# A decoder layer in float32: the embedding's product moved ahead of the up projection, and sixteen tiles used twice

## The chip, the core and the metric

The kernel runs on one core of a Trainium2 chip. Its engines work side by side, each through a list of instructions of its own: TensorE (PE) multiplies matrices, with weight loads shown apart as PEld; VectorE (DVE), ScalarE (ACT) and GpSimd (POOL) work on elements; SyncE (SP) starts transfers, and ACT starts some too. An instruction waits until what it needs has been produced and until the place it writes is free. On chip the data lie in 128 partitions: SBUF for operands, PSUM in eight banks for the sums of PE. The metric is the time of one execution on the device in microseconds, the median of several; a profiled execution gives the trace.

## What is computed

One layer of a decoder trunk over 1024 positions and 1024 channels: a mixer of three head groups, a gated feed-forward part, an embedding gated into the stream, and norms:

```python
h = h + jnp.concatenate([o_a, o_b.astype(o_a.dtype), o_c.astype(o_a.dtype)], axis=-1) @ w_out[l]
h = h + conv_glu_ffn(rmsnorm(h, norm_ffn_g[l]), ffn_up[l], ffn_conv_w[l], ffn_conv_b[l], ffn_down[l])
gate = jax.nn.sigmoid(rmsnorm(h, norm_ple_g[l]) @ ple_gate[l])
h = h + gate * (p[l] @ ple_proj[l])
```

`conv_glu_ffn` projects up to 2 x 2816 columns, runs a causal convolution of width 3, multiplies the SiLU of one half with the other half, and projects down. `p[l] @ ple_proj[l]`, the embedding's product (256 channels to 1024), depends on nothing that the layer computes; the last line alone needs it.

## The kernel before

All data are float32, with channels on partitions and positions along the free axis, in two halves of 512 positions (`hf` 0 and 1). Each operand of a product is split into a rounded high part and the rest as a low part (`split2`, `split_x`, `op_split`: a cast on ACT, a subtraction on DVE or POOL), and each product is three matmuls: high by high, high by low, low by high (`mm3`, L127, L129, L131; `mul`, L1094). A matmul takes 128x128 weights and 512 moving columns.

The kernel is a sequence of stages, written with pools of tiles. A pool's tiles take addresses in SBUF from the lower side, or, with `side="right"`, from the upper side. A tile that lies over an older one waits for the last use of that one. A planner of the language puts the instructions of each engine into their final order from the order of the program, the dependencies and its own idea of their durations; on the chip each engine then keeps that order. The stages that the change touches:

- **Out projection** (`phase_out`). The mixer's output stands split in the X tiles (32 of 512 columns, both halves, one pool `x`). For each half and each of eight row blocks m, the weights are loaded through the ring `wraw` (two slots, shared), split, and multiplied (`dense`, 24 matmuls to a half). DVE adds the sum to h (L1073), ACT stores it (L1074), ACT squares it and DVE adds the squares to `acc` (`sq_acc`, L185 to L189). Row blocks 0 and 1 do both halves at once. After each half `rstd_bcast` adds up over partitions by small matmuls (L159), takes the power -1/2 on POOL (L167) and spreads the result by transposes into a PSUM tile (L169).
- **Passage** (`ffn_norm`, `ffn_operands`). The up projection works by a scheme that replaces eight block products by seven, so its moving operands are seven sets of four blocks, p1 to p7, each split in high and low: p1 and p2 are the first half of the normalised h; the others are sums and differences of all blocks. `ffn_norm` scales both halves (L1122) and splits p1 and p2 (L1112, L1113). Their tiles, pool `tx`, lie where the X tiles were. `ffn_operands` loads the weights of the first two units, loads and splits the embedding's inputs through `wraw` (L1143 to L1148), multiplies p1 for two units (bank tiles `bg`), copies the result to `e` (L1201), multiplies p2 on top, and then computes the embedding's product in eight blocks of 12 matmuls (bank tiles `bv`), each copied to SBUF (L1167) and stored to memory (`ped`, L1168). Behind these in the program stand the sums and splits of p6, p5, p7 (L1175 to L1189), and of p3 and p4, whose pool `ty` lies over the embedding's tiles.
- **Up projection** (`phase_up`). 22 units, each with the products p6, p4, p5, p2, p7, p3 and p1 in pairs; its results are convolved, gated and stored.
- **Down projection** (`phase_down`). Seven products of eleven steps by the same scheme. Each step loads a block (`xs`, six tiles), splits it into two of eight tiles `xb` (dx in the profile), and takes weights (`S`, `W1`, `W2`). They all lie in pools opened when the up projection's are closed.
- **Last stage** (`ple_norm`, `phase_ple`). The gate's product, eight row blocks by two halves, with the first half's operands in a pool on the upper side and the second half's on the lower. Each row block reads back its part of `ped`.

Of the kernel before, what the change touches and what calls it, by code (L numbers as in the profile page):

```python
# [18 lines left out]
P = 128  # L19
# [60 lines left out]
class Trunk:  # L80
# [57 lines left out]
    def xall(self):  # L138

        X = [({}, {}) for _ in range(ND)]  # L140
        for h in (1, 0):
            for k in range(ND):
                X[k][0][h] = self.xpool.tile([P, HT], F32R, tag=f"xh{k}_{h}", name=self.nm("xh"), bufs=1)
                X[k][1][h] = self.xpool.tile([P, HT], F32R, tag=f"xl{k}_{h}", name=self.nm("xl"), bufs=1)
        return X
# [54 lines left out]
    def build(self):  # L200
        tc, nc = self.tc, self.nc
        with ExitStack() as st:
# [5 lines left out]
            mix, psm = ExitStack(), ExitStack()  # L208
            self.xpool = mix.enter_context(self.pool("x"))
# [15 lines left out]
            with self.pool("fps", bufs=2, space=PSUM) as self.fps:  # L225
                self.ffn_operands(hs, up)
                self.phase_up()
                up.close()
                with ExitStack() as ple:
# [824 lines left out]
    def phase_out(self, hp, op):  # L1054
# [5 lines left out]
        pbs = []  # L1060
        for hf in (0, 1):
            sl = slice(hf * HT, (hf + 1) * HT)
            acc = op.tile([P, HT], F32, tag="acc", name=self.nm("acc"))
            for m in range(ND):
                t = self.h[m][:, sl]
                if m > 1 or hf == 0:
                    w = self.load_w(self.a["w_out"][m])
                    ps = self.dps.tile([P, T], F32, tag="dp", name=self.nm("dp"))
                    halves = (0, 1) if m < 2 else (hf,)
                    self.dense([ps[:, :HT], ps[:, HT:]], w, self.O, (6, 7, 0, 1, 4, 2, 3, 5), halves)  # L1070
                    for g in halves:
                        u = self.h[m][:, g * HT:(g + 1) * HT]
                        nc.vector.tensor_tensor(u, u, ps[:, g * HT:(g + 1) * HT], ALU.add)  # L1073
                        nc.scalar.dma_start(self.hd[m][g], u)  # L1074
                self.sq_acc(acc, t, m == 0)
            pbs.append(self.rstd_bcast(acc, 1.0 / 1024, EPS, self.mxp))
        return pbs
# [37 lines left out]
    def ffn_norm(self, pbs):  # L1115

        self.TX = {}
        self.op_tiles(self.tpool, "p7", "p6", "p1", "p2", "p5")
        for hf in (0, 1):
            for k in (0, 1, 2, 3, 4, 5, 6, 7) if hf == 0 else (0, 4, 1, 5, 2, 6, 3, 7):  # L1120
                t = self.h[k][:, hf * HT:(hf + 1) * HT]
                self.nc.vector.scalar_tensor_tensor(t, t, self.par[:, PC_FFN + k:PC_FFN + k + 1], pbs[hf],  # L1122
                                                    ALU.mult, ALU.mult)
                if hf == 0:
                    self.op_split("p2" if k >= 4 else "p1", k % 4, t)

    def ffn_operands(self, hs, up):


# [3 lines left out]
        self.units = [{"f": f} for f in range(NFF)]  # L1133
        first = self.units[:2]
        for d in first:
            d["raw"], d["rav"] = self.load_up(d["f"]), self.load_up(NFF + d["f"])
            d["w1"] = self.split2(d["raw"][:, :HT], V)
        with self.pool("pe") as pp:
            pX, pw = [], []
            for k in (0, 1):  # L1140
# [416 lines left out]
```

## Time and profile before

| | us |
|---|---|
| three executions | 1567.61, 1567.92, 1576.19 |
| their median | 1567.92 |
| the profiled execution | 1568.74 |
| its span, first to last instruction | 1567.0 |

The profile shows one execution. Its page has the busy time of each engine and its share of the span. The timeline has a line for each run of like instructions: start, duration, engine (a q behind it marks the queue that issues transfers), the line in the source, output and inputs by the program's names, size and count, and in brackets how long the engine had stood idle and what ended that. PE's matmuls overlap: each is shown with 0.39 us, and at full pace one starts every 0.2267 us, so pace is read from starts. In the view by stretches each line has the stretch, its length, the busy time of PE, PEld, DVE, ACT and POOL with the number of instructions, the TensorE clock that was granted (1.00 is full), the share of time that DMA was busy, and GB/s.

### The profile page before, as it was taken

What the parts mean: (1) busy time and instruction counts of PE and PEld (TensorE: products, weight loads), DVE (VectorE), ACT (ScalarE), POOL (GpSimd) and SP (SyncE); (2) the same over time, 40 slices, a digit from 0 to 9 for tenths busy, and PEclk for the clock granted to TensorE, in tenths of its full rate; (3) what the DMA queues carried; (4) which work ended last, traced back from release to release, by engine and by line L of the source; (5) the groups of instructions that cost most, each with busy time, mean ns of one, the idle gap of its engine ahead of it and who ended that gap; (6) DMA issues with size and microseconds to landing.
All of it is one profiled execution on the core that took longest, in us unless ns stands there. A gap on an engine that the chain in (4) does not pass through costs nothing.

```text
span 1567.0 us, 20112 instructions
## 1 busy us (share of the span) xinstructions
PE 1488.1 (95%) x7480; PEld 1225.3 (78%) x7480; DVE 1098.7 (70%) x1578; ACT 631.1 (40%) x1079; POOL 430.5 (27%) x353
## 2 busy tenths in 40 slices
PE   7999999999999988999889999999999999999995
PEld 5778988788877777777768888888888778888774
DVE  6567542756556568844758888888888789867584
ACT  6522421312324455523445444444444444455541
POOL 2233220313211123213124455444454000002230
PEclk9999999989999999999989999999999999999998
DMA  5124002124043032054332333333331793352352
GB/s 193 58 88 121 28 28 81 41 74 108 1 147 103 28 108 75 28 202 148 121 120 95 101 104 111 103 103 108 107 111 70 251 329 106 112 156 61 101 175 81
DMA packets 78707, 167.84 MB, mean 107 GB/s; under 512 B 19920, under 2 KB 20048, under 8 KB 78608
## 3 DMA queue, kind: packets, MB, share of 16 engines
q1 hardware_dynamic: 65120, 145.97, 28.7%
q10 hardware_dynamic: 12400, 16.52, 3.1%
q0 software_dynamic: 1088, 4.06, 0.8%
q8 instruction: 59, 0.97, 0.3%
q14 instruction: 40, 0.33, 0.1%
HBM read 120.12 MB, written 46.40 MB: 106 GB/s over the span
## 4 chain that ended last, share of the span: by engine, by line
PE 67%; issue 18%; DVE 8%; ACT 3%; DMA 2%; POOL 1%; POOLq 0%; SPq 0%; ACTq 0%; DVEq 0%
PE bg L1094 15%; PE bv L1094 11%; PE dp L131 6%; PE dp L129 6%; PE dp L127 6%; PE hsc L849 1%; PE swq L993 1%; PE pgm L743 1%; PE bv L131 1%; PE bv L129 1%; PE bv L127 1%; PE sc L560 1%; PE swt L1016 1%; PE swo L1029 1%; PE px L736 1%
## 5 line engine op out<-in xcount | busy, mean ns | idle before, releaser
L127 PE MATMUL dp<-xh,whi 128*128 128x512 f32 x544 | 185.3, 399 | 12.7 <-ACT xh L344 8.6
L129 PE MATMUL dp<-xl,whi 128*128 128x512 f32 x544 | 186.0, 399 | 0.4 <-DVE xl L345 0.3
L131 PE MATMUL dp<-xh,wlo 128*128 128x512 f32 x544 | 184.2, 397 | 1.0 <-POOL wlo L106 1.0
L106 POOL TENSOR_TENSOR wlo<-raw,whi 128x512 fp32r<-128x512 f32 x84 | 134.9, 1623 | 92.8 <-ACT whi L104 92.7
L104 ACT CAST whi<-wraw 128x512 fp32r<-128x512 f32 x120 | 73.2, 619 | 210.4 <-PE dp L129 144.5
L106 POOL TENSOR_TENSOR wlo<-wraw,whi 128x512 fp32r<-128x512 f32 x60 | 82.5, 1375 | 269.7 <-ACT whi L104 253.2
L127 PEld LDWEIGHTS dp<-xh,whi 128*128 128x128 f32 x544 | 102.4, 190 | 36.0 <-ACT xh L344 8.6
L131 PEld LDWEIGHTS dp<-xh,wlo 128*128 128x128 f32 x544 | 103.4, 191 | 23.4 <-POOL wlo L106 1.9
L129 PEld LDWEIGHTS dp<-xl,whi 128*128 128x128 f32 x544 | 102.7, 190 | 24.3 <-DVE xl L345 2.6
L106 POOL TENSOR_TENSOR wlo<-s,whi 128x512 fp32r<-128x512 f32 x44 | 68.3, 1552 | 163.2 <-ACT whi L104 148.9
L1403 PE MATMUL bg<-dx,whi 128*128 128x512 f32 x308 | 96.6, 394 | 1.7 <-DVE dx L1400 1.5
L1403 PE MATMUL bv<-dx,whi 128*128 128x512 f32 x308 | 95.0, 390 | 0.0
L104 ACT CAST whi<-raw 128x512 fp32r<-128x512 f32 x88 | 52.5, 619 | 100.6 <-issue 51.1
L104 ACT CAST whi<-s 128x512 fp32r<-128x512 f32 x66 | 39.0, 620 | 115.3 <-PE bg L1094 112.1
L106 DVE TENSOR_TENSOR wlo<-wraw,whi 128x512 fp32r<-128x512 f32 x60 | 46.5, 780 | 49.1 <-ACT whi L104 44.3
L167 POOL TENSOR_TENSOR rst<-rst,mhalf 128x4 f32<-128x4 f32 x8 | 9.3, 1160 | 255.6 <-DVE rst L161 255.6
L1403 PEld LDWEIGHTS bg<-dx,whi 128*128 128x128 f32 x308 | 56.8, 188 | 17.5 <-ACT whi L104 4.1
L1403 PEld LDWEIGHTS bv<-dx,whi 128*128 128x128 f32 x308 | 57.8, 188 | 12.2
L1399 ACT CAST dx<-xraw 128x512 fp32r<-128x512 f32 x77 | 47.9, 622 | 46.1 <-PE bv L1403 24.8
L1400 DVE TENSOR_TENSOR dx<-xraw,dx 128x512 fp32r<-128x512 f32 x77 | 54.8, 712 | 3.0 <-ACT dx L1399 2.7
L1403 PE MATMUL bg<-dx,wlo 128*128 128x512 f32 x154 | 47.5, 390 | 1.1 <-DVE wlo L106 1.1
L286 DVE TENSOR_TENSOR dp<-dp,rstd 128x512 f32<-128x512 f32 (+1 forms) x26 | 23.3, 898 | 35.5 <-PE dp L131 25.5
(404 smaller groups left out, 3874.6 us busy)
## 6 DMA issues: line engine op xcount, KB each, us to landing
raw<-in_ffn_up_dram SPq DMA_DIRECT2D x44, 512.0 KB, 3.7
wraw<-in_w_in_dram SPq DMA_DIRECT2D x30, 512.0 KB, 3.7
z<-zst SPq DMA_DIRECT2D x18, 512.0 KB, 3.1
gb<-ct SPq DMA_DIRECT2D x33, 256.0 KB, 2.0
xraw<-gb SPq DMA_DIRECT2D x33, 256.0 KB, 2.9
xraw<-gt SPq DMA_DIRECT2D x33, 256.0 KB, 2.7
zl<-z SPq DMA_DIRECT2D x16, 512.0 KB, 3.9
wraw<-in_ple_gate_dram SPq DMA_DIRECT2D x16, 512.0 KB, 3.6
```

Of the source, the lines that this page charges most:

```text
L104: nc.scalar.copy(hi, src)
L106: eng.tensor_tensor(lo, src, hi.bitcast(F32), ALU.subtract)
L127: nc.tensor.matmul(ps[hf], wh, xh[hf], start=first, stop=False)
L129: nc.tensor.matmul(ps[hf], wh, xl[hf], start=False, stop=False)
L131: nc.tensor.matmul(ps[hf], wl, xh[hf], start=False, stop=last)
L286: self.nc.vector.tensor_tensor(ps, ps, r, ALU.mult)
L560: nc.tensor.matmul(ps[:, u, :], bb[:, u, :, :].rearrange("p a b -> p (a b)"), d["ar"][:, 4 * g + u, 0, :], start=True, stop=True)
L736: nc.tensor.matmul(px[:, u, :], U[:, 2 * hh + u, :], Xr[:, 2 * hh + u, :], start=True, stop=True)
L1094: nc.tensor.matmul(ps, w[part == 2][:, s], X[k][part == 1], start=start and k == part == 0, stop=k == 3 and part == 2, skip_group_check=no ...
L1399: nc.scalar.copy(xh, x)
L1400: V.tensor_tensor(xl, x, xh.bitcast(F32), ALU.subtract)
L1403: nc.tensor.matmul(ps[m], wt[part == 2][:, m * P:(m + 1) * P], (xh, xl)[part == 1], start=k == part == 0, stop=k == NK - 1 and part == 2)
```

## The change

**Pools.** The X tiles get one pool for each half, `x1` below `x0`. On the upper side a tile of 24 floats, `edge`, comes first, and a pool `t16` of sixteen tiles of 512 columns next; all other pools of the upper side follow behind them, lower than before.

```diff
-            self.xpool = mix.enter_context(self.pool("x"))
+            psm = ExitStack()
+            mix = [ExitStack(), ExitStack()]
+            self.xpool = [None, mix[1].enter_context(self.pool("x1"))]
+            self.xpool[0] = mix[0].enter_context(self.pool("x0"))
...
+            e(self.pool("edge", side="right")).tile([P, 24], F32, name="edge")
+            self.t16 = e(self.pool("t16", side="right"))
             up, hs = ExitStack(), ExitStack()
...
-            pbs = self.phase_out(hp, mix.enter_context(self.pool("acc")))
-            mix.close()
-            self.tpool = up.enter_context(self.pool("tx"))
-            self.ffn_norm(pbs)
+            emb = ExitStack()
+            self.pxp = emb.enter_context(self.pool("px", side="right"))
+            pb = self.phase_out(hp, mix[0], emb)
+            self.ffn_norm(1, pb)
             psm.close()
+            for n, ks in (("p6", range(4)), ("p5", range(4, ND))):
+                self.TX[n] = [[self.xpool[1].tile([P, HT], F32R, tag=f"x{c}{k}", name=f"t{n}{c}{k}", bufs=1) for c in "hl"]
+                              for k in ks]
```

**Tiles by generations.** p1 and p2 lie in `t16`, p6 and p5 in the second half's X tiles. In the down projection the sixteen tiles are used again: p1's for the six `xs` and for `S[0]`, `S[1]`, p2's for the eight `xb`.

```diff
+        xs = [self.tile16(i, F32) for i in range(6)]
+        S = {k: self.tile16(6 + k, F32) for k in (0, 1)}
+        xb = [self.tile16(8 + i, F32R) for i in range(8)]
         wa = aa.enter_context(self.pool("wa", side="right"))
-        xr = ple.enter_context(self.pool("xr"))
...
+        xl = ple.enter_context(self.pool("xl"))
+        for k in range(2, NK):
+            S[k] = xl.tile([P, HT], F32, name=f"sr{k}")
```

**Out projection.** The first half's rows come first, then one row block of the second half, then the first half's rstd. The other five row blocks of the second half have the first half's normalisation and its splits into p1 and p2 between them, two steps to a row block, and the four loads and splits of the embedding's inputs (`pe_load`), through a ring of their own with two slots. The second half's squares follow behind all rows, then its rstd, the loads of the first up weights, and five of the eight blocks of the embedding's product in the out projection's banks.

```diff
+        for m in range(ND):
+            rows(m, (0, 1) if m < 2 else (0,))
+            self.sq_acc(acc, self.h[m][:, :HT], m == 0)
+        rows(2, (1,))
+        pb = self.rstd_bcast(acc, 1.0 / 1024, EPS, self.mxp)
+        x0.close()
+        self.TX = {}
+        for i, n in enumerate(("p1", "p2")):
+            self.TX[n] = [[self.tile16(8 * i + 2 * k + c, F32R) for c in (0, 1)] for k in range(4)]
...
+        norm = self.ffn_norm(0, pb)
+        for m in range(3, ND):
+            rows(m, (1,))
+            for _ in range(2):
+                next(norm, None)
+            if parts:
+                self.pe_load(pwp, *parts.pop(0))
+        for m in range(ND):
+            self.sq_acc(acc, self.h[m][:, HT:], m == 0)
+        pb = self.rstd_bcast(acc, 1.0 / 1024, EPS, self.mxp)
+        self.ffn_first()
+        for m in range(5):
+            self.embed(m, pw, px, self.dps.tile([P, T], F32, tag="dp", name=self.nm("dp")))
+        self.pe_in = (pw, px)
+        return pb
+
+    def embed(self, m, pw, px, ps):
...
+        t = self.wpool.tile([P, T], F32, tag="wraw", name=self.nm("pst"), bufs=2)
+        self.nc.scalar.copy(t, ps)
+        self.nc.scalar.dma_start(self.ped[m], t)
...
+    def pe_load(self, raws, dst, pool, src, k):
+        raw = raws.tile([P, T], F32, tag="praw", name=self.nm("praw"), bufs=2)
+        self.nc.sync.dma_start(raw, self.a[src][k])
```

**Passage.** The sums and splits of p6 and p5 stand first, then the last three embedding blocks, then the products with p1 and p2 of the first two units; p7, p3 and p4 follow, with all three in the pool `ty`.

```diff
         for k in range(4):
             split("p5", k, B11[k])
+        for d in first:
+            d["G"] = self.banks("g")
+        for m in range(5, ND):
+            self.embed(m, *self.pe_in, self.banks("v"))
+        self.mul(*[(d["G"][:, :HT], d["w1"], self.TX["p1"], True) for d in first])
+        for d in first:
+            self.keep_first(d)
+        for d in first:
+            d["w2"] = self.split2(d["raw"][:, HT:], V)
+        self.mul(*[(d["G"][:, :HT], d["w2"], self.TX["p2"], False) for d in first])
         for k in range(4):
             V.tensor_tensor(B12[k], B22[k], B12[k], ALU.subtract)
-            split("p7", k, B12[k])
-        self.op_tiles(up.enter_context(self.pool("ty")), "p4", "p3")
...
+        emb.close()
+        pool = up.enter_context(self.pool("ty"))
+        self.op_tiles(pool, "p3", "p7", "p4")
```

The arithmetic is the same: no product, sum or transfer is added or dropped.

More of the change, by code (lines that the diff above doesn't have):

```diff
@@ L1077, in phase_out, with rows @@
-        return pbs
+        acc = hp.tile([P, HT], F32, name="acc")
+        def rows(m, halves):
+            w = self.load_w(self.a["w_out"][m])
+            ps = self.dps.tile([P, T], F32, tag="dp", name=self.nm("dp"))
+            self.dense([ps[:, :HT], ps[:, HT:]], w, self.O, (6, 7, 0, 1, 4, 2, 3, 5), halves)
+            for g in halves:
+                u = self.h[m][:, g * HT:(g + 1) * HT]
+                nc.vector.tensor_tensor(u, u, ps[:, g * HT:(g + 1) * HT], ALU.add)
+                nc.scalar.dma_start(self.hd[m][g], u)
@@ L1258, in unit @@
                 conv(prev, 0)
-            d["V"] = self.banks("v")
+            if "V" not in d:
+                d["V"] = self.banks("v")
             jobs = [(d["V"][:, :HT], ws["6"], TX["p6"], True)]
```

117 lines of the change are left out of this document (40 added, 77 removed).

## The prediction

> **What bounds the kernel now.** I read the page's shares first, then the chain of waits, then busy time by stretches, then the timeline of the stretch that stands out.
>
> ```profile
> PE 1488.1 (95%) x7480; PEld 1225.3 (78%) x7480; DVE 1098.7 (70%) x1578; ACT 631.1 (40%) x1079; POOL 430.5 (27%) x353
> ```
>
> TensorE (PE) bounds the program: a change pays only where PE stands still or runs slow. The stretches around the passage from the out projection to the up projection:
>
> ```profile
> core 0: us, PE busy (x) PEld busy (x) DVE busy (x) ACT busy (x) POOL busy (x), PEclk, DMA share, GB/s
> 742.64:769.86 27.22, 27.22 (x121) 22.34 (x119) 20.43 (x31) 13.43 (x23) 3.91 (x4) 1.00 0.45 145
> 769.86:801.25 31.39, 18.57 (x66) 14.54 (x65) 27.72 (x44) 13.19 (x24) 9.58 (x4) 0.73 0.08 25
> 801.25:822.26 21.01, 21.01 (x94) 17.43 (x93) 6.37 (x9) 9.59 (x12) 2.60 (x2) 1.00 0.57 216
> 822.26:1230.13 407.87, 407.87 (x1801) 337.46 (x1800) 355.01 (x366) 172.76 (x241) 191.50 (x123) 1.00 0.31 102
> ```
>
> The last five output rows (first line) and the whole up projection (last line: 1801 matmuls in 407.87 us, 0.2265 us each) leave PE no hole. The second line is the hole: PE busy 18.57 of 31.39 us at a granted clock of 0.73, while VectorE (DVE) works 27.72. Its timeline on PE:
>
> ```profile
> 769.63 0.39 PE L131 MATMUL dp<-xh,wlo 128*128 128x512 f32 x1
> 773.64 1.25 PE L159 MATMUL ps_ss<-few,acc 128*128 128x1 f32 x8 [3.62 <-DVE acc L189]
> 776.61 1.11 PE L169 MATMUL ps_ss<-cst,rst 128*128 128x128 f32 x4 [1.72 <-POOL rst L167]
> 777.38 1.20 PE L1094 MATMUL bg<-tp1h,whi 128*128 128x512 f32 x2
> ...
> 785.32 0.70 PE L127 MATMUL bv<-pxh,pwh 128*128 128x512 f32 x2 [0.47 <-DVE h L1122]
> ...
> 793.50 0.79 PE L1094 MATMUL bg<-tp2h,whi 128*128 128x512 f32 x1 [7.01 <-ACT e L1201]
> ...
> 801.25 0.61 PE L131 MATMUL bv<-pxh,pwl 128*128 128x512 f32 x2
> ...
> 822.10 0.39 PE L1094 MATMUL bv<-tp6h,whi 128*128 128x512 f32 x1
> ```
>
> From the last matmul of the rows (769.63) to the first with p6 (822.10) are 52.47 us. They hold that matmul, 24 with p1, 24 with p2 and 96 of the embedding: 145 x 0.2267 = 32.87. So 19.6 us are lost: the wait for the sum of squares, for the spread of rstd, for the copy of e, and matmuls at a low clock after each (p2: 24 in 7.75 us, 5.44 at full pace). Call 769.86, where the rows' last slot ends, E.
>
> **The change part by part.**
>
> *The embedding's product moves ahead, p1 and p2 behind it.* Before, p1 and p2 lie over the rows' operands, so they are split only when the rows have ended, and DVE does that ahead of the second half's normalisation:
>
> ```profile
> 775.01 2.49 DVE L1113 TENSOR_TENSOR tp1l<-h,tp1h 128x512 fp32r<-128x512 f32 x4
> 777.41 2.49 DVE L1113 TENSOR_TENSOR tp2l<-h,tp2h 128x512 fp32r<-128x512 f32 x4
> 779.82 5.34 DVE L1122 SCALAR_TENSOR_TENSOR h<-h,par,ps_ss 128x512 f32<-128x512 f32 x8
> 785.09 1.28 DVE L1179 TENSOR_TENSOR h<-h 128x512 f32<-128x512 f32 x2
> ...
> 794.72 0.68 DVE L1113 TENSOR_TENSOR tp6l<-nu,tp6h 128x512 fp32r<-128x512 f32 x1
> ```
>
> After, they have tiles of their own, and the splits run within the rows. DVE there is busy 20.43 of 27.22 us; 4.98 come in: 25.4, it still fits. Behind E: the spread arrives at 776.61 + 1.11 = E+7.9 as now, the normalisation begins at once instead of at 779.82 and ends at E+13.2, and the 10.3 us of sums and splits from 785.09 to 795.40 give p6 at E+23.5. PE has at E, ready, the five embedding blocks (60 matmuls, 13.6 us), then three more (8.2) and p1 and p2 (10.9): 32.6 us. p6 is wanted at E+32.6 at the earliest and is there 9 us before. So the filler covers the whole chain, and the 3.62 us wait goes; what is late next is not p6 but small things in PE's order, each of which I price:
>
> - *Spread of rstd.* It stays, within running matmuls. The first half's shows the cost:
>
> ```profile
> 737.81 0.39 PE L129 MATMUL dp<-xl,whi 128*128 128x512 f32 x1
> 738.04 0.94 PE L159 MATMUL ps_ss<-few,acc 128*128 128x1 f32 x8
> ...
> 740.33 0.65 PE L169 MATMUL ps_ss<-cst,rst 128*128 128x128 f32 x4 [0.76 <-POOL rst L167]
> 740.74 0.48 PE L129 MATMUL dp<-xl,whi 128*128 128x512 f32 x1
> ```
>
> Three slots after 737.81 would be 738.49; it is 740.74: 2.3 us. Without its wait of 0.76 it would be 1.5, with today's wait of 1.72 at this place 3.2. I take 2.3, the same kind of place.
>
> - *Copy of e.* It stands between p1 and p2, as before, and ACT takes its work in the order in which it was laid out:
>
> ```profile
> 785.86 1.17 ACT L1112 CAST tp5h<-h 128x512 fp32r<-128x512 f32 x2 [9.93 <-DVE h L1179]
> 792.87 1.06 ACT L1201 COPY e<-bg 128x512 f32<-128x512 f32 x2
> ```
>
> Today PE waits 7.0 us for it, because ACT stands behind casts that wait for DVE, which is late. After, p1 starts when the eight blocks are through (E + 13.6 + 8.2 + 2.3 = E+24.1) and ends at E+29.5; DVE is through p6 and p5 (E+23.5 and four more splits, 2.5) by then, so ACT should be free. The two copies alone are 1.06. From 0 (other matmuls lie between) to 7.0; I take 1.5.
>
> - *Bank of embedding block 5.* It takes a bank that the spread's result used until E+13.2; PE comes there at E+13.6+2.3. Today's wait for the same thing is 0.47 (785.32). From 0 to 3; I take 0.5.
>
> - *DVE in the rows.* The last sums of squares now stand behind all rows in the program, and 25.4 of 27.2 us is nearly full:
>
> ```profile
> L1148 DVE TENSOR_TENSOR pxl<-wraw,pxh 128x512 fp32r<-128x512 f32 x4 | 3.3, 855 | 0.0
> L1148 DVE TENSOR_TENSOR pwl<-wraw,pwh 128x512 fp32r<-128x512 f32 x4 | 2.7, 688 | 3.3 <-ACT pwh L1147 3.3
> ```
>
> The same subtraction takes 0.688 us and, where POOL is at work too, 0.855. If POOL's 3.91 us in the window came on top, DVE would be 2.1 us late at E. Up to 9 us late is covered; a matmul placed too early waits for it. From 0 to 3; I take 1.0.
>
> Sum: 2.3 + 1.5 + 0.5 + 1.0 = 5.3 us stay of 19.6. Gain 14.3.
>
> *Own loads.* The embedding's inputs leave the weights' ring for a ring of their own on the same queue (SP): the same four loads. No price; PE has no wait in those rows today. The four loads of the first up weights move too: their tiles now lie where the mix phase still works, so they leave SP after 671.47, and have some 100 us until p1 wants them. The embedding's eight copies (1.02 each) and stores sit on ACT from E on instead of from 803; ACT is busy 13.19 of the 31.39 us there, so they fit. The output tiles h lie lower in memory and may come later; today they are issued last in the mix phase:
>
> ```profile
> 671.47 1.76 SPq L1103 DMA_DIRECT2D raw<-in_ffn_up_dram  x4
> ...
> 685.70 3.94 ACTq L1059 DMA_DIRECT2D h<-in_xT_dram  x8
> 690.24 1.28 DVE L1073 TENSOR_TENSOR h<-h,dp 128x512 f32<-128x512 f32 x2 [2.67 <-PE dp L131]
> 706.58 0.50 PE L127 MATMUL dp<-xh,whi 128*128 128x512 f32 x1 [2.32 <-ACT whi L104]
> ...
> 803.26 1.02 ACT L1167 COPY pst<-bv 128x1024 f32<-128x1024 f32 x1 [0.78 <-PE bv L131]
> ```
>
> The first sum waits for PE, not for h; a delay of 2 us is hidden by the second row's matmuls, as the two rows' banks take turns. The wait at 706.58 comes from ACT's order; from 3 us less to 3 more, I take 0.
>
> *Tiles aligned.* The timeline shows a reason in the last stage, where the first half's operands lie on the upper side and the second half's on the lower:
>
> ```profile
> 1447.98:1459.22 11.24, 11.24 (x49) 9.04 (x48) 4.30 (x7) 4.38 (x6) 4.24 (x3) 1.00 0.45 148
> 1497.84:1508.49 10.65, 10.65 (x48) 8.82 (x47) 9.41 (x12) 5.02 (x9) 3.53 (x3) 1.00 0.62 210
> ```
>
> Both stretches run from one matmul's start to another's: 48 steps of 0.2342 us in the first, 47 of 0.2266 in the second, at the same clock. If the upper side's offset is the cause, 8 x 24 = 192 matmuls gain 0.0076: 1.4 us. From 0 to that; I take 1.4, since at the same clock nothing but the side differs to the first one's harm: DVE and the DMA are busier in the second.
>
> *Sixteen shared tiles.* p1 and p2 give their places to the down projection's inputs:
>
> ```profile
> 1221.75 0.39 PE L1094 MATMUL bg<-tp2h,wlo 128*128 128x512 f32 x1
> 1224.58 0.38 SPq L1397 DMA_DIRECT2D xraw<-gb  x1
> 1227.45 0.62 ACT L1399 CAST dx<-xraw 128x512 fp32r<-128x512 f32 x1 [8.40 <-DMA xraw<-gb]
> ```
>
> p2 is read last at 1221.75; the first load is issued at 1224.58 and the first cast into a shared tile stands at 1227.45, held by the load. No new wait: 0, from 1 less to 2 more.
>
> All: 14.3 + 1.4 = 15.7. The profiled execution took 1568.74 (span 1567.0), 0.8 above the median: 1553.0 by it, 1552.2 by the median, and I give that.
>
> **The rivals.**
>
> *Nothing but the spread stays.* The three small waits fall under other matmuls, and the row's wait of 2.32 goes too: 19.6 - 1.5 + 1.4 + 2.3 = 21.8, 1546.1; without the row 1548.4. For: p6 is 9 us early. Against: every in-order wait above has a precedent.
>
> *The alignment does nothing.* If the pace in the last stage has another cause than the offset, such as POOL, a little busier there (4.24 of 11.24 against 3.53 of 10.65), 14.3 remain: 1553.6. Against: in the up projection POOL is busy 191.50 of 407.87 and the pace is 0.2265. [...]
>
> *The order turns against it.* ACT again stands behind casts, e is waited for 7.0 us, and p2 runs cold (7.75 for 5.44): 2.3 + 7.0 + 2.3 + 1.0 = 12.6 stay; gain 7.0 + 1.4 = 8.4, 1559.5. For: the present order, laid out ahead by a planner, puts four embedding matmuls before p2 (785.32 to 786.5) where the wait had room for 31 more. Against: DVE is now done with those splits before p1 ends.
>
> *The alignment goes the wrong way.* If the 96 bytes put the upper side off instead of on, p1 and p2 (22 x 24 = 528), the embedding (96) and the down projection's inputs (7 x 11 x 12 = 924) run at 0.2342: 1548 x 0.0076 = 11.8 lost, nothing gained in the last stage: 1567.92 - 14.3 + 11.8 = 1565.4. The change would then not do what it says.
>
> *Slower: weights starve.* The embedding's loads have two slots; the third waits on SP until DVE has split the first, with output weights queued behind it. If each of four loads costs PE a row of 24 matmuls, 21.8 us are lost: 1567.92 - 15.7 + 21.8 = 1574.0. It decides from 3.9 us per load on. Against: the same loads pass today without a wait.
>
> **How the numbers follow.** Forecast 0.44 (own range 1549 to 1556), only the spread 0.15, alignment for nothing 0.06, the order 0.25, alignment the wrong way 0.05, starving 0.05. The range 1547.5 to 1562 leaves out half of the second case and the last two: 0.18. One per cent, about what a measurement tells from no change, is 15.7 us: 1552.2. Faster: the second case and just over half of the first (0.25), 0.40. Slower by over 1%, above 1583.6: starving half as bad again, 0.02. The rest, 0.58.
>
> **What would show it.** Embedding matmuls straight behind the last row at clock 1.0; p1 and p2 split among the rows; the normalisation right behind the spread; 0.2266 in the last stage's first half; no new wait at 1230. A wait of several us before p2 or at the sum of squares speaks for the order; any wait among the rows for starving; a pace of 0.234 in the up projection against the alignment.

## The result, and the profile after

| | before | after |
|---|---|---|
| executions | 1567.61, 1567.92, 1568.28, 1576.19 | 1551.12, 1550.87, 1548.9, 1550.8 |
| median | 1568.1 | 1550.84 |
| the profiled execution's span | 1567.0 | 1549.3 |

The ratio of the means is 0.9875 (95% interval 0.9842 to 0.9908): 1.25% less. The median is 1.4 us under the forecast of 1552.2. Where the time went is another matter. The view by stretches, cut at the same events in both kernels: the end of the mix phase, the end of the rows, the first matmul with p5, the first of the down projection, the first of the last stage, the end. Columns as in the prediction. The kernel before:

```profile
core 0: us, PE busy (x) PEld busy (x) DVE busy (x) ACT busy (x) POOL busy (x), PEclk, DMA share, GB/s
0.00:684.38 684.38, 645.56 (x3807) 536.54 (x3808) 414.18 (x716) 254.92 (x501) 170.53 (x183) 0.97 0.24 79
684.38:769.86 85.48, 81.68 (x363) 66.15 (x361) 43.15 (x63) 30.64 (x52) 16.99 (x14) 1.00 0.52 176
769.86:824.82 54.96, 42.13 (x169) 34.07 (x169) 35.04 (x55) 25.30 (x40) 12.19 (x6) 0.84 0.29 102
824.82:1230.13 405.31, 405.31 (x1789) 335.36 (x1788) 354.06 (x365) 170.24 (x238) 191.50 (x123) 1.00 0.31 102
1230.13:1447.98 217.85, 214.61 (x937) 173.75 (x937) 178.69 (x282) 106.61 (x177) 10.45 (x7) 1.00 0.53 172
1447.98:1566.97 118.99, 98.77 (x421) 79.39 (x419) 73.61 (x101) 43.42 (x74) 28.85 (x21) 0.90 0.37 121
```

The changed kernel:

```profile
0.00:679.45 679.45, 642.63 (x3807) 533.63 (x3807) 408.20 (x713) 254.82 (x501) 169.03 (x183) 0.98 0.24 78
679.45:763.04 83.59, 81.59 (x365) 66.59 (x364) 49.74 (x74) 34.97 (x60) 17.00 (x14) 1.00 0.55 193
763.04:802.84 39.80, 37.87 (x170) 30.34 (x168) 31.60 (x50) 22.39 (x35) 5.01 (x4) 1.00 0.43 152
802.84:1218.06 415.22, 413.31 (x1790) 336.71 (x1789) 362.30 (x369) 172.06 (x239) 196.79 (x126) 1.00 0.32 105
1218.06:1431.62 213.56, 213.11 (x938) 174.74 (x936) 174.83 (x275) 102.54 (x170) 10.51 (x7) 1.00 0.51 163
1431.62:1549.35 117.73, 96.70 (x421) 77.98 (x419) 73.68 (x101) 43.22 (x74) 28.90 (x21) 0.91 0.37 122
```

Line by line: mix phase -4.93, rows -1.89, passage -15.16, up projection **+9.91**, down projection -4.29, last stage -1.26; together -17.62. Behind the mix phase it is 882.59 to 869.90: -12.69, where 15.7 were forecast. The mix phase holds no edit. In the up projection PE is as full as before and has the same matmuls (1789, 1790), and still needs 413.31 us for 405.31: its matmuls are slower, and there is a hole of 1.9.

The passage on PE, in the timeline of the changed kernel:

```profile
762.81 0.39 PE L131 MATMUL dp<-xh,wlo 128*128 128x512 f32 x1
763.04 0.63 PE L127 MATMUL dp<-peh,peh 128*128 128x512 f32 x2
...
766.90 1.02 PE L159 MATMUL ps_ss<-few,acc 128*128 128x1 f32 x8 [0.48 <-DVE acc L189]
...
769.26 0.65 PE L169 MATMUL ps_ss<-cst,rst 128*128 128x128 f32 x4 [0.77 <-POOL rst L167]
...
786.42 0.74 PE L127 MATMUL bv<-peh,peh 128*128 128x512 f32 x2 [0.69 <-ACT pst L1118]
...
794.56 0.40 PE L1148 MATMUL bv<-tp6h,whi 128*128 128x512 f32 x1
...
808.06 0.39 PE L1148 MATMUL bv<-tp7h,wlo 128*128 128x512 f32 x1
810.36 0.47 PE L1148 MATMUL bg<-tp3h,whi 128*128 128x512 f32 x1 [1.91 <-ACT whi L104]
```

The embedding stands straight behind the last row; the waits of 3.62 and 7.01 are gone. New is the wait of 1.91 ahead of the first p3; behind it seven steps from start to start take 0.43 instead of 0.2267, and the granted clock from 811.90 to 815.10 is 0.50 (called half clock below). On DVE:

```profile
739.34 1.89 DVE L1167 TENSOR_TENSOR t<-h,t 128x512 fp32r<-128x512 f32 x3
...
769.95 5.36 DVE L1174 SCALAR_TENSOR_TENSOR h<-h,par,ps_ss 128x512 f32<-128x512 f32 x8 [1.83 <-PE ps_ss L169]
...
785.49 0.68 DVE L1167 TENSOR_TENSOR tp6l<-nu,tp6h 128x512 fp32r<-128x512 f32 x1
...
807.84 1.77 DVE L1262 TENSOR_TENSOR s<-s,raw 128x512 f32<-128x512 f32 x1 [1.54 <-POOL wlo L106]
809.53 0.67 DVE L1311 TENSOR_TENSOR x<-e,bg 128x512 f32<-128x512 f32 x1
```

And on ACT, the copies of the blocks 5 and 6 and the cast of p3's weights:

```profile
785.36 1.92 ACT L1118 COPY pst<-bv 128x1024 f32<-128x1024 f32 x2
...
809.70 0.62 ACT L104 CAST whi<-s 128x512 fp32r<-128x512 f32 x1 [2.14 <-DVE s L1262]
```

p1's splits run among the rows (739), the normalisation starts right behind the spread, and p6 is ready at 786.17, 23.1 us behind the rows' end (forecast 23.5); PE takes it at 794.56 (31.5, forecast 32.6).

### The profile page after: what moved, and what is told of

Its sections match the earlier page's. It is cut to its first block, busy times and chain, and to the rows that moved or that the text cites. A ratio compares the mean times of both kernels' runs of the same rounds, so it can differ in the third digit from the quotient of the medians.

```text
span 1549.3 us, 20120 instructions
## 1 busy us (share of the span) xinstructions
PE 1485.2 (96%) x7480; PEld 1220.0 (79%) x7480; DVE 1100.4 (71%) x1578; ACT 630.0 (41%) x1079; POOL 427.2 (28%) x353
## 4 chain that ended last, share of the span: by engine, by line
PE 80%; DVE 7%; issue 5%; ACT 3%; POOL 2%; DMA 2%; POOLq 0%; SPq 0%; ACTq 0%; DVEq 0%
PE bg L1148 15%; PE bv L1148 11%; PE bv L1439 7%; PE bg L1439 7%; PE dp L131 7%; PE dp L129 7%; PE dp L127 7%; PE hsc L857 2%; PE swq L1001 1%; PE pgm L751 1%; PE swo L1037 1%; PE swt L1024 1%; PE zp L127 1%; PE zp L129 1%; PE zp L131 1%
## 5 line engine op out<-in xcount | busy, mean ns | idle before, releaser
L104 ACT CAST whi<-wraw 128x512 fp32r<-128x512 f32 x120 | 73.3, 619 | 203.7 <-PE dp L129 141.7
L1148 PE MATMUL bg<-t,whi 128*128 128x512 f32 x352 | 134.3, 392 | 0.0
L1439 PE MATMUL bv<-t,whi 128*128 128x512 f32 x308 | 95.7, 392 | 0.0
L1439 PE MATMUL bg<-t,whi 128*128 128x512 f32 x308 | 95.7, 391 | 0.0
L104 ACT CAST whi<-raw 128x512 fp32r<-128x512 f32 x88 | 52.5, 618 | 98.6 <-issue 52.0
L104 ACT CAST whi<-s 128x512 fp32r<-128x512 f32 x66 | 38.8, 619 | 126.1 <-PE bg L1148 122.5
L1148 PEld LDWEIGHTS bg<-t,whi 128*128 128x128 f32 x352 | 66.2, 188 | 14.7
L1148 PE MATMUL bg<-t,wlo 128*128 128x512 f32 x176 | 67.8, 392 | 0.0
L1439 PEld LDWEIGHTS bg<-t,whi 128*128 128x128 f32 x308 | 57.8, 188 | 12.6
L1439 PEld LDWEIGHTS bv<-t,whi 128*128 128x128 f32 x308 | 57.9, 188 | 12.4
L1435 ACT CAST t<-t 128x512 fp32r<-128x512 f32 x77 | 47.7, 621 | 48.4 <-PE bv L1439 34.7
```

Of the source, the lines that this page charges most:

```text
L104: nc.scalar.copy(hi, src)
L1148: nc.tensor.matmul(ps, w[part == 2][:, s], X[k][part == 1], start=start and k == part == 0, stop=k == 3 and part == 2, skip_group_check=no ...
L1435: nc.scalar.copy(xh, x)
L1439: nc.tensor.matmul(ps[m], wt[part == 2][:, m * P:(m + 1) * P], (xh, xl)[part == 1], start=k == part == 0, stop=k == NK - 1 and part == 2)
```

## The experiments

All were timed against runs of the kernel before on the same chip. The rows come from several chips, so the ratios can be compared with each other and the medians only roughly. Since the mix phase differs from profile to profile with no edit in it, stages are compared from its end on, each from one profile. The two profiles of the changed kernel agree within 0.25 us in every stage behind it. Small differences of the last stage mean little: it takes 117.7 to 119.2 us in kernels whose first half runs at the same pace there (changed, old order).

| kernel | median, us | ratio to before (95%) | rows' end to first p5 | up | down | last | mix end to end |
|---|---|---|---|---|---|---|---|
| before | 1568.1 | 1 | 54.96 | 405.31 | 217.85 | 118.99 | 882.59 |
| changed | 1550.84 | 0.9875 (0.9842 to 0.9908) | 39.80 | 415.22 | 213.56 | 117.73 | 869.90 |
| edge of 8 floats | 1551.16 | 0.9889 (0.9855 to 0.9922) | 40.07 | 411.14 | 217.59 | 117.97 | 870.33 |
| no edge | 1557.58 | 0.9923 (0.9895 to 0.9952) | 40.18 | 415.96 | 218.47 | 117.67 | 875.89 |
| lower side 64 down | 1555.38 | 0.9897 (0.9855 to 0.9938) | 40.10 | 411.12 | 217.58 | 118.66 | 871.10 |
| before, with edge | 1567.0 | 0.9989 (0.9972 to 1.0006) | 55.83 | 405.33 | 217.82 | 118.45 | 884.51 |
| edge of 40 floats | 1542.51 | 0.9815 (0.9792 to 0.9838) | 39.57 | 409.11 | 211.49 | 117.33 | 861.17 |
| own tile for s3 | 1545.93 | 0.9829 (0.9798 to 0.9861) | 38.97 | 408.76 | 211.51 | 117.80 | 860.69 |
| old order | 1565.48 | 0.9959 (0.9942 to 0.9977) | 53.07 | 415.37 | 213.55 | 119.20 | 884.83 |
| split inputs low | 1550.44 | 0.9868 (0.9842 to 0.9894) | 39.78 | 414.24 | 211.51 | 118.87 | 867.99 |
| p6 ahead | 1546.19 | 0.9846 (0.9815 to 0.9878) | 39.55 | 407.84 | 211.51 | 118.43 | 860.98 |
| raw inputs late | 1545.54 | 0.9847 (0.9818 to 0.9876) | 39.55 | 408.11 | 212.43 | 117.50 | 861.22 |
| changed, again | 1551.26 | 0.9892 (0.9856 to 0.9927) | 39.81 | 415.20 | 213.55 | 117.98 | 870.15 |

**Where the upper side starts.** Three kernels shift one side against the other, and one gives the kernel before the edge alone.

```diff
-            e(self.pool("edge", side="right")).tile([P, 24], F32, name="edge")
+            e(self.pool("edge", side="right")).tile([P, 8], F32, name="edge")
```

> The changed kernel with the upper side pushed down by 32 bytes instead of 96: its tiles then start 64 bytes past a multiple of 128, as the lower side's tiles do, instead of on a multiple of 128. Theory A (the offset of the operands sets TensorE's pace): every step of 512 columns at 0.2267 us in the up projection (now up to 0.2314), the embedding (0.2295), the down projection (0.2287) and the last stage's first half (0.2289); about 6.6 + 0.3 + 1.9 + 0.4 = 9.2 us less, 1541.6. Theory B (operands on the upper side are slower than the old ones for another reason, such as height or the tiles' order): paces as in the changed kernel, 1550.8, within 1.

Without the edge (the line is taken out):

> The changed kernel without the 96 bytes: upper tiles start 32 bytes past a multiple of 64, as before the change. Theory A: 0.234 in the last stage's first half, as before, and now also with p1, p2 and the operands of the down projection that lie on the upper side, above 0.2314; some 6 to 9 us more, 1557 to 1560. Theory B: the last stage's first half alone goes back to 0.234 (1.0 more) and the rest stays: 1551.8.

The lower side, 64 bytes down:

```diff
-        r = self.spool.tile([P, 4], F32, tag="rst", name=self.nm("rst"), bufs=2)
+        r = self.spool.tile([P, 4], F32, tag="rst", name=self.nm("rst"), bufs=1)
...
-        r2 = self.spool.tile([P, 4], F32, tag="rst2", name=self.nm("rst2"), bufs=2)
+        r2 = self.spool.tile([P, 4], F32, tag="rst2", name=self.nm("rst2"), bufs=1)
```

> The changed kernel with one buffer instead of two for the two small tiles of rstd at the start of the lower side: everything above them on that side, the weights among it, lies 64 bytes lower and so starts on a multiple of 128, as the upper side's tiles do. Theory A1 (an operand must start 64 bytes past a multiple of 128): all streams at 0.2289 or slower, the mix phase and the rows too, 1556 or more. Theory A2 (the moving operand must have the same offset as the weights): all at 0.2267, 1541.6. Theory B: paces as in the changed kernel, 1550.8. The second rstd of a pair waits for the first; at most 0.5 us.

The kernel before, with the edge of 24 floats ahead of its upper pools:

> The kernel before with the 96 bytes alone. Both theories of the pace: the last stage's first half at 0.2289 instead of 0.2342, 1.0 us less, 1566.9; nothing else has fast operands on the upper side there. The mix phase (end of its last transposes at 684.38 before, 679.45 after the change, with no edit in it): if the 4.9 us there come from the layout of the upper side, this run shows 679.5 and some 1562; if from what is issued ahead of or behind the mix phase, or from chance in the clock, 684 and 1566.9.

None of the theories on the pace holds as it stood. The first half's 48 matmuls in the last stage of the kernel before with the edge:

```profile
1445.52:1456.50 10.98, 10.98 (x49) 9.01 (x48) 4.31 (x7) 4.38 (x6) 4.30 (x3) 1.00 0.44 146
```

0.2288 each, from 0.2342, as in the changed kernel and as both theories had it: there the edge alone sets the pace. The edge of 8 and the lowered lower side agree to 0.02 us in the up and down projections, though in one all tiles start 64 bytes past a multiple of 128 and in the other on it: the absolute start does not matter (A1 falls), nor is an equal offset modulo 128 enough (A2 falls). B falls too, as the paces change with the shift. What the two share is the distance between the sides.

**Distance 0.** The same line with 40 floats.

> The changed kernel with the upper side pushed down by 160 bytes instead of 96. The runs so far have upper tiles at these distances from the lower side's places, modulo 2048 bytes: 64 (changed kernel; up projection 0.2302 us a matmul, down 0.2288), 128 (the edge of 8 floats and the lowered lower side, alike in every stage: p1 and p2 0.234, everything else of the up projection 0.2263, down 0.2333), 160 (no edge: 0.2310, 0.2343). Here the distance is 0, as between all tiles of the lower side. Theory A, now: the distance modulo 2048 (or a divisor of it over 128) between the moving operand and the weights sets the pace, and 0 is free: 0.2267 in every stage, up projection 6 to 7 us shorter than in the changed kernel, down 1.9, last stage 0.4; 1541.5. Theory B, that operands on the upper side are slower wherever they start: p1 and p2 at 0.230 or more, 1549 to 1552.

One unit of the up projection, 84 matmuls from the first p3 to the end of p7, in the view by stretches: before, changed, and edge of 40.

```profile
920.05:939.09 19.04, 19.04 (x85) 15.77 (x84) 16.20 (x17) 7.91 (x12) 9.43 (x7) 1.00 0.26 83
```

```profile
922.42:941.76 19.34, 19.34 (x85) 15.76 (x84) 17.66 (x19) 7.90 (x12) 9.49 (x7) 1.00 0.38 123
```

```profile
921.60:940.64 19.04, 19.04 (x86) 15.77 (x84) 17.46 (x19) 7.91 (x12) 9.41 (x7) 1.00 0.37 125
```

At the same clock the changed kernel needs 0.30 us more a unit; at distance 0 that is gone, with DVE and DMA as busy as before the shift. A's forecast for distance 0 holds: 8.7 us less behind the mix phase. By its median this is the fastest kernel of the study; three kernels below that build on it lie within 0.5 us of it behind the mix phase.

**The pace by itself.** This program computes nothing of the layer: 48 matmuls for each of 17 distances, nothing beside them, then four checks of side and weights.

```diff
+        for j, (x, v, i) in enumerate(seq):
+            k = i % 4
+            nc.tensor.matmul(ps[:, j % 2 * HT:(j % 2 + 1) * HT], v[:, k * P:(k + 1) * P], x, start=j < 2,
+                             stop=j >= len(seq) - 2)
```

> A program of its own, which computes nothing of the layer: one set of 128x512 weights, and streams of 48 matmuls, each on one moving tile that starts a set distance past the weights' place modulo 2048 bytes (0 to 1984), nothing else running; at the end two tiles on the upper side (distances 0 and 64, some 210,000 bytes up), then weights 64 bytes further with the moving tiles of 64 and 0. Theory A (distance between moving tile and weights): 0.2267 at 0, about 0.229 at 64, 0.233 at 128, 0.234 at 160, slower at 64 than at 0 on the upper side too, fast again for the tile of 64 with the moved weights. Theory C (what costs is a matmul whose moving tile starts elsewhere than that of the one before it): 0.2267 in every stream but for its first step. Theory D (only with other traffic on SBUF): 0.2267 everywhere.

Its timeline: xa lies at distance 0 from wx, xb 32, xc 64, xd 96, xe 128, xf 160, xg 192, xi 256, xj 320, xk 384; xy and xz on the upper side at 0 and 64; wy 64 past wx.

```profile
62.95 11.37 PE L1614 MATMUL acc<-xb,wx 128*128 128x512 f32 x48
74.16 11.16 PE L1614 MATMUL acc<-xc,wx 128*128 128x512 f32 x48
85.15 11.37 PE L1614 MATMUL acc<-xd,wx 128*128 128x512 f32 x48
96.36 11.36 PE L1614 MATMUL acc<-xe,wx 128*128 128x512 f32 x48
107.56 11.40 PE L1614 MATMUL acc<-xf,wx 128*128 128x512 f32 x48
118.80 11.35 PE L1614 MATMUL acc<-xg,wx 128*128 128x512 f32 x48
...
141.19 11.05 PE L1614 MATMUL acc<-xi,wx 128*128 128x512 f32 x48
152.07 11.17 PE L1614 MATMUL acc<-xj,wx 128*128 128x512 f32 x48
163.07 11.32 PE L1614 MATMUL acc<-xk,wx 128*128 128x512 f32 x48
...
240.38 11.06 PE L1614 MATMUL acc<-xy,wx 128*128 128x512 f32 x48
251.28 11.17 PE L1614 MATMUL acc<-xz,wx 128*128 128x512 f32 x48
262.29 11.05 PE L1614 MATMUL acc<-xc,wy 128*128 128x512 f32 x48
273.18 11.36 PE L1614 MATMUL acc<-xa,wy 128*128 128x512 f32 x48
284.38 11.07 PE L1614 MATMUL acc<-xa,wx 128*128 128x512 f32 x48
```

From start to next start: 10.88 us at 256 (0.2267 a matmul), 11.00 at 320 and 10.99 at 64 (0.229), 11.21 at 32 (0.2335), 11.20 at 128 (0.2333), 11.24 at 160 (0.2342). The upper side is no slower than the lower (10.90 at 0, 11.01 at 64), and the tile xc, slow with wx, is fast with the moved weights (10.89). So for a stream with one moving tile it is the distance between that tile and the weights, modulo 256: A holds, D falls, and C falls as the whole cause. Stages whose moving tiles all lie at one distance show the same numbers: 160 in the last stage's first half before the change (0.2342) and in the down projection without the edge (218.47 us), 64 in the last stage's first half (0.2288) and the down projection of the changed kernel (213.56 us).

The up projection isn't given by this table. There p1 alternates with p3, and p2 with p5, and p3 to p7 stay at distance 0. A unit has 24 matmuls with p1 and p2. At the paces of the pace run they would add 0.06 us to the 19.04 of distance 0 at 64, 0.16 at 128 and 0.18 at 160. Measured are 19.34 at 64 (0.30 more), 19.21 and 19.20 at 128 (edge of 8, lowered lower side: 0.17 and 0.16) and 19.45 at 160 (no edge: 0.41). At 64, the stretches of 24 steps with p1 or p2 take 5.55 or 5.56 instead of 5.44; p6 with p4 take 5.48 instead of 5.44, and p7 2.76 instead of 2.72, though p4, p6 and p7 lie at distance 0. So the slower stream of p1 and p2 accounts for 0.06 of the 0.30 us a unit, and the edge of 8, whose distance is the slower one in the pace run, has the shorter up projection (411.14 for 415.22). Part of it may be seen in the pace run: behind a change of the moving tile a stream of 48 at distance 0 takes from 10.88 us (xi behind xh) to 10.93 (xl behind xk), up to 0.05 over 48 x 0.2267; where in the stream is not shown. So C may have a share. Why alternation costs more at 64 and 160 than at 128 stays open; that distance 0 is free (10.88 us for 48, and 19.04 a unit as before the change) is shown in both.

**The order of the filler.** All eight embedding blocks back behind p2, everything else as changed (the first five thereby move to the bank tiles of the other three).

```diff
-        for m in range(5, ND):
-            self.embed(m, *self.pe_in, self.banks("v"))
         self.mul(*[(d["G"][:, :HT], d["w1"], self.TX["p1"], True) for d in first])
...
         self.mul(*[(d["G"][:, :HT], d["w2"], self.TX["p2"], False) for d in first])
+        for m in range(ND):
+            self.embed(m, *self.pe_in, self.banks("v"))
```

> The changed kernel with its embedding blocks back behind p1 and p2, as before the change; early splits of p1 and p2, loads, tiles and alignment stay. Theory (the filler's place matters): behind the last row p1 follows, its two products end 10.9 us later, e is waited for, p6 is ready 23.5 us behind the rows at the earliest and 32.9 us of matmuls stand ahead of it, so it isn't waited for; what is lost anew is the wait for e between p1 and p2 and the clock behind it, 3 to 9 us from the rows' end to the first p5 over the 39.8 us of the changed kernel. Rival (the early splits alone did it, the place of the filler is free): 39.8 within 1.5.

53.07 us from the rows' end to the first p5 over 39.80: 13.3 lost, more than the theory asked for, and the rival falls. Its waits on PE:

```profile
766.89 1.48 PE L159 MATMUL ps_ss<-few,acc 128*128 128x1 f32 x8 [3.63 <-DVE acc L189]
769.71 1.11 PE L169 MATMUL ps_ss<-cst,rst 128*128 128x128 f32 x4 [1.34 <-POOL rst L167]
784.55 1.22 PE L1146 MATMUL bg<-t,whi 128*128 128x512 f32 x2 [5.72 <-ACT e L1234]
```

The waits of before are nearly all back. The early splits and tiles are worth 54.96 - 53.07 = 1.9 us by themselves (one profile each; the kernel before with the edge shows 55.83); the rest of the passage's gain hangs on work that is ready standing behind the rows.

**The hole ahead of p3.** The sum x reads the bank that p3 adds to, and stands on DVE behind the sum L1262 (807.84), which waits for POOL. The same sum makes p3's weights: ACT casts it from 809.70 to 810.32, x ends at 810.20, and p3 starts at 810.36. Two remedies, on the edge of 40: s3 in a tile of its own, and the second unit's p6 ahead of p3.

```diff
-                V.tensor_tensor(d["s"]["3"], d["s"]["3"], d["s"]["2"], ALU.add)
+                s3 = cv.tile([P, HT], F32, tag="s3", name=self.nm("s3"), bufs=1)
+                V.tensor_tensor(s3, d["s"]["3"], d["s"]["2"], ALU.add)
+                d["s"]["3"] = s3
```

> As the run with 160 bytes, and the third weight sum of a unit gets a tile of its own instead of being written over the sixth's. In the changed kernel the first p3 matmul stands 1.9 us behind p7 and then runs at half clock for 3 us; the sum x, which must read the bank ahead of it, stands on DVE behind that third sum, which waits for POOL to have split the sixth. Theory (order on DVE): without that wait x is done by the end of p7, the first p3 follows within 0.3 us, no half clock, 3 to 4 us less from the first p6 to the second unit's p5 than in the run with 160 bytes; some 1538. Rival (PE waits for POOL's or ACT's split of the weights themselves): the gap moves to the next product and at most 1 us goes.

```diff
+            if prev and not new:
+                d["V"] = self.banks("v")
+                self.mul((d["V"][:, :HT], ws["6"], TX["p6"], True))
```

> The run with 160 bytes, and for the second unit alone the twelve matmuls with p6 are put ahead of the first unit's p3. In the runs so far PE stands 1.7 to 1.9 us behind the first p7, because the sum x, which reads the bank that p3 adds to, comes late on DVE, behind the second unit's weight sums; a tile of its own for one of these took the wait off DVE but the sums themselves then filled the time. Theory: the second unit's p6 weights are split by the time p7 ends (POOL ends them 0.3 us before), so the twelve matmuls (2.7 us) fill the gap; x is done within them; no half clock behind. 1.9 + 1.6 = 3.5 us less than with 160 bytes alone, 1539.0. Rival: DVE is still late for what follows (p4 needs the sum behind x), and the gap moves there: 1541 to 1543.

Neither brought its 3 to 4 us (up projection 408.76 and 407.84 over 409.11). With the tile of its own DVE no longer waits, but the sums ahead of x fill the time, and PE still waits 1.72:

```profile
811.25 1.78 DVE L1257 TENSOR_TENSOR raw<-raw 128x512 f32<-128x512 f32 x1
812.95 1.77 DVE L1263 TENSOR_TENSOR s<-s,raw 128x512 f32<-128x512 f32 x1
814.64 0.67 DVE L1313 TENSOR_TENSOR x<-e,bg 128x512 f32<-128x512 f32 x1
```

With p6 ahead the hole splits in two, and the profile now names DVE:

```profile
822.21 0.50 PE L1148 MATMUL bv<-tp4h,whi 128*128 128x512 f32 x1 [1.04 <-DVE bv L1316]
...
831.57 0.47 PE L1148 MATMUL bg<-tp3h,whi 128*128 128x512 f32 x1 [0.87 <-DVE x L1314]
```

So the hole hangs on DVE's order: with p6 ahead the waits name DVE's sums, and they stand at p4 and at the next unit's p3, as the second rival had it. In the changed kernel, and with the tile of its own, two things stand between DVE's sum and p3: ACT's cast of p3's weights and x. They end within 0.12 us of each other (with the tile of its own at 815.42 and 815.31), so the runs don't tell which of them PE waits for. Of the 1.3 us that went with p6 ahead, 1.0 is the half clock's: the kernel with the raw inputs late (below) has the order of the edge of 40 in this stage and the same hole (1.94 in both), but no half clock (mean clock 1.00 over 24 us, 0.93 with the edge of 40), and takes 408.11. Against that, p6 ahead gains 0.27 and the tile of its own loses 0.65.

**The start of the down projection.** Before the change SP issued the first loads behind stores of the last units that wait for DVE:

```profile
1210.95 0.32 SPq L1312 DMA_DIRECT2D gt<-t  x1
1222.97 0.32 SPq L1298 DMA_DIRECT2D gb<-ct  x1
1224.17 0.32 SPq L1312 DMA_DIRECT2D gt<-t  x1
1224.58 0.38 SPq L1397 DMA_DIRECT2D xraw<-gb  x1
```

In the changed kernel they are issued 21 us ahead of the stage's first matmul (1218.06), not 5.6:

```profile
1197.11 0.32 SPq L1433 DMA_DIRECT2D t<-gb  x1
...
1198.97 0.86 SPq L1433 DMA_DIRECT2D t<-gb  x2
```

First, the split inputs on the lower side again:

```diff
-        xb = [self.tile16(8 + i, F32R) for i in range(8)]
+        S.update({2 + i: self.tile16(8 + i, F32) for i in range(8)})
...
+        xb = [xl.tile([P, HT], F32R, name=f"dx{i}") for i in range(8)]
```

> The changed kernel with the eight split inputs of the down projection back on the lower side, over the places of p6, and eight of its weight blocks in the sixteen shared tiles in their place. Theory A: all of the down projection at 0.2267 instead of 0.2288, 1.9 us less. Start of the stage: before the change PE waited there for the input's split 1.47 us and for the weights' 1.11, and ran cold behind; in the changed kernel it doesn't. If that came from the inputs' tiles being free early (sharing), the waits come back, 3 to 6 us, and the stage takes 214.7 to 218 us from its first matmul to the last stage's; if it came from somewhere else (loads issued earlier, DVE's order), 211.7.

211.51: the pace is back (distance 0) and no wait is. Where the split inputs lie is not the cause. Then, on the edge of 40, the raw inputs in p2's tiles:

```diff
-        xs = [self.tile16(i, F32) for i in range(6)]
+        xs = [self.tile16(8 + i, F32) for i in range(6)]
```

> The run with 160 bytes, with the sixteen shared tiles dealt out the other way: the down projection's raw inputs in p2's tiles, which the last unit reads 8.4 us before the stage, and its split inputs in p1's, which are free some 22 us before. Theory (the raw inputs' early tiles are what took the stage's first waits away): their loads are issued behind p2's last matmul, as before the change, the first splits are late again, and the down projection takes 214 to 218 us from its first matmul to the last stage's first, over 211.5 in the run with 160 bytes. Rival (the weights' early loads, or DVE's order): 211.5 within 0.7.

The loads came 12.5 us ahead of the stage (1200.43 for 1212.93), not as late as intended, and it took 212.43, 0.9 over the edge of 40. Loads 5.6 us ahead go with 6.4 lost, 12.5 with 0.9, 21 with nothing. But where the time is lost fits the raw inputs' lead only in part. Before the change the steps over 0.2267 add up to 3.5 us in the first 12 us of the stage, at two waits (1.11 for a weights' low part, 1.47 for an input's), and to 2.8 between 22 and 62 us into it, where PE waits for ACT's casts of the weights (L104). With the raw inputs late, nothing is lost in the first 22 us, and the 0.9 lies at those casts. So the weights' sums, whose loads moved too, have a share. A run with the lead of before was not made; which loads took the first two waits away stays open.

**The mix phase.**

> The changed kernel once more, unchanged. In eleven profiles of kernels with one and the same mix phase its last transposes stood between 679.45 and 688.49, with stretches of half clock of different lengths before them. If that is chance of the clock, the same kernel shows another number than its 679.45 here, anywhere up to 689, and 869.9 within 0.7 from there to the end; if it belongs to what a kernel has behind that phase, 679.45 within 0.5 again. Time 1550.8, up to 1555.

680.83 where 679.45 stood; behind it 870.15. The phase, with no edit in any of these kernels, ended between 679.45 and 688.49 (edge of 8), and at 679.46 in the kernel before with the edge alone. So its 4.93 us cannot be put down to the change. Whether the kernel before sits at 684 by chance of the clock or by something that no view shows stays open.

## Why the prediction was right, and where its sum was wrong

The time was right; the sum was right only because its errors cancel, and because the mix phase, which belongs to no step, ended 4.9 us earlier. With the mix phase of the profile before, the profiled execution would have taken 1551.12 + 4.93 = 1556.1, 3.0 over the 1553.0 that the prediction gives by the profile. That the forecast came so close is luck.

- *The filler* is the mechanism, and the runs show it (old order: 13.3 us). 19.6 us lost between the rows' end and p5 became 39.80 - 156 x 0.2267 = 4.4; 5.3 were forecast to stay. Spread of rstd: 2.3 taken, with DVE's 1.0; together 3.0 by the steps from 766.03 to 769.99. (The 0.855 that DVE's price was read from is a mean of three subtractions at 0.68 and one at 1.38.) Bank of block 5: 0.5 taken, nothing lost; it starts at 779.84 without a wait. What costs 1.0 is the bank of block 7 (786.42): ACT copies block 5 out of it only behind its casts for p5 and p6. The rest is pace. Copy of e: 1.5 taken, nothing lost, since the first p6 matmuls stand between p1 and p2.
- *"What is late next"* was answered with small things in PE's order up to p2. It missed the first p3: 1.91 of wait and 1.6 of half clock (seven steps, 0.2 each, and two half ones). The up projection at distance 0 takes 409.11 over 405.31, so 3.8 us, or 2.8 where no half clock follows (408.11). The prediction stopped its list at p2; the sums of the second unit, which DVE had to do somewhere, came due behind it.
- *Tiles aligned.* 1.4 taken; 48 matmuls of the last stage's first half take 10.98 us for 11.24 (0.2288, not the 0.2266 looked for), 1.0 over all 192 (the prediction's 192 x 0.0076 is 1.5); the stage is 1.26 shorter, which its scatter doesn't tell from 1.0. What failed is the other half of the step: it saw 0.2342 on the upper side, laid it to the offset, and then priced p1, p2 and the down projection's inputs, which move to that side, as if 96 bytes settled it. They move from distance 0 to 64: 415.22 - 409.11 = 6.1 us in the up projection and 213.56 - 211.49 = 2.1 in the down projection. The 2.1 are 924 matmuls at 0.229; of the 6.1 the 528 matmuls with p1 and p2 give 1.2 at that pace, and the rest lies in the stretches that they share with p3 and p5 and in the products at distance 0 behind these. The rival of the wrong way, at 0.05, had the right place, with 11.8 us for 8.2, and the wrong reason: without the 96 bytes it is 6.0 worse still.
- *Alignment does nothing* fell: with the 96 bytes the last stage's pace changed from 0.2342 to 0.2288, in the kernel before with the edge alone too.
- *Shared tiles*, 0 (from 1 less to 2 more): 6.4 us gained (217.85 to 211.49 at equal pace). The step asked only for new waits and took the row quoted, the first load at 1224.58, as none; it didn't ask which old waits would go. Two waits behind 1230 (3.5) and the small ones behind the weights' casts (2.8) went. That earlier loads are the reason is argued from their lead and not shown apart for inputs and weights.
- *Rows*, 0 within 3: 1.9 gained, with a wait of 1.53 in place of 2.32 and 0.67; not tested. *Own loads*: no wait in the rows showed; starving fell.
- *The order turns against it* (0.25) did not come, but the old-order run shows that its wait was real: 5.72 of 7.0 for e, with ACT behind casts that wait for DVE. In the changed kernel the same order of ACT costs the 1.0 at block 7.

Behind the mix phase 12.7 came of 15.7; the mix phase gave 4.9 that belong to no step.

## What to carry to other kernels

Fill a wait with work that is ready by placing it where the wait is: here the same 96 matmuls were worth 13 us straight behind the rows and nothing behind p1 and p2. When operands change their side or place, price the pace of all their matmuls and of those that alternate with them, and look at the distance between moving tile and weights. And follow a filled gap to the next instruction that DVE had no room for, and early loads to the stage that they feed: with the pace, these were the large errors of the sum.

## What the runs showed of the hardware

- The pace of a stream of 128x512 matmuls in this type depends on the distance between the moving tile's start and the weights' modulo 256 bytes. In the pace run, with nothing beside them in the program, a matmul takes 0.2267 to 0.2277 us at 0 (10.88 to 10.93 for 48, at 256, 512, 1024 and 1536), 0.229 at 64, and 0.232 to 0.234 at 32, 96, 128, 160, 192 and 224. The same moving tile takes 10.99 us for 48 with one place of the weights and 10.89 with another, so the weights' place matters to the running matmuls; by what way is not shown.
- Products at distance 0 were slower behind streams with tiles at 64: in the changed kernel p7, all at distance 0 and behind p2 and p5, takes 2.76 us for 12 (0.2300). Where tiles at two distances alternate, the two paces together give a unit's time at 128 (19.20 for 19.20 and 19.21) and too little at 64 (19.10 for 19.34) and 160 (19.22 for 19.45); why is open.
- After a hole ahead of p3 of 1.91 us in the changed kernel the granted clock was 0.50 from 811.90 to 815.10; with the edge of 40, after 1.94, seven steps take 0.43, with a mean clock of 0.93 over 24 us. After one of 1.94 at the same place with the raw inputs late, and of 1.89 with the split inputs low, the mean clock over 24 us was 1.00. So the hole's length alone does not decide it; what does is not shown.
